# Split weight sums of two pairs of both wide gates formed ahead and kept; weighing of the attention on ScalarE; adds of the output stage's jobs behind the spreading of queries

## The chip, the cores and the metric

One NeuronCore of a Trainium2 chip. The metric is device time of one execution in microseconds (us), median of several. The engines of the core: PE (TensorE, matmuls; PEld is its weight loading), DVE (VectorE), ACT (ScalarE), POOL (GpSimd) and SP (SyncE), which issues most of the DMA transfers. PSUM, where matmuls write, has eight banks of 128x512 floats, here all given out by one pool ("bank").

## The reference

One layer of an encoder on 256 tokens of width 2048, in float32:

```python
h = rms_norm(x, norm_mix)
uv, qkv, gates = split(h @ w_in)
u, v = split(gelu(uv));  v = layer_norm(v)
y_a = u * (w_s @ v + b_s)                   # 8 groups, chunks of 128 tokens
y_b = neighbourhood_attention(q, k, v, rpb) # 16 heads of 64
g_a, g_b = split(sigmoid(gates))            # 2 x 2048 columns
x = x + (g_a * (y_a @ wb_a) + g_b * (y_b @ wb_b)) @ w_out
x = x + (silu(gate) * val) @ w_down         # gate, val: convolved h2 @ w_up, 2 x 5504 columns
out = rms_norm(x, norm_final)
```

## The kernel before

**Numbers.** A float32 value is written as a high and a low part (type fp32r). A product of a piece takes three matmuls: high by high, low by high, high by low. The weights come from DRAM in full and are split in the kernel: ACT copies the high part (`whi`, L165), DVE subtracts it (`wlo`, L166).

**Pieces.** The program goes through some 470 pieces of weights of 256 rows, in a list. `begin(i)` opens piece i: it issues the load of piece i+5 on SP's queue (five raw buffers), splits piece i+3 (four buffers), and then runs the tasks that were hung on number i with `at(i, f)`, those of the construction first. The order of the instructions on every engine is the order in which this Python runs; nothing is reordered, and an engine that waits holds up all that is behind it. So the numbers handed to `at` are the schedule.

**Groups around the change.** v and the attention's v (pieces 0 to 31, wide), u (32 to 47), then by turns a group of q and k (8 pieces, two pairs of heads) and one of a half gate (8 pieces): 48 to 111. Four half branches (112 to 127, four pieces each), the wide halves of gate A (128 to 143) and of gate B (144 to 159), the last branches (160 to 175), the output projection (176 to 207), and then up and down.

**Wide groups and quads.** A wide group has 16 pieces of 256 rows by 512, in eight pairs; a pair is a 256x1024 block of weights. It is worked off plainly (24 matmuls, 2 pieces of 4 products) or as a quad, by block sums that need seven products instead of eight (21 matmuls; 9 in the first piece, 12 in the second). For a quad, four sums of the activations' blocks and four of the weights' blocks must be formed on DVE and split on ACT and DVE. `GATE_QUADS` says which positions of a gate's order are quads, `GATE_ORDER` which rows stand where. A wide group takes four banks for plain products (`C`), and from its first quad on four more for the quads' own products (`P`). In the output stage the split weight sums of some pairs are formed far ahead ("jobs", `split_ahead`): a load `tw` of 1 MB on SP's queue, four adds of 128x512 on DVE (L1226), two splits of 128x1024 (ACT L1231, DVE L1232), and four writes of 512 KB to DRAM, from where they are read back by `split_read` on POOL's queue.

**Mixing.** In the u group, `mix` has PE multiply v into a bank (tasks of pieces 43 to 46 and 51 to 54); DVE adds the bias from it (L684), multiplies u (L685) and splits the result with ACT (L531, L532).

**Attention.** For each pair of heads, in steps hung on piece i: `scores` on PE (L815) from `qs`, `ks` and the low part `kl` that the spreading of queries leaves (DVE L743, L744); one piece later the exponential on ACT (L838); then `weigh`, the division by the sum (DVE L846); at i+5 `turn`, four transpositions on PE (L855) that ACT copies out; at i+8 `apply`.

**Merging.** `ev_branch` multiplies a branch with its gate on DVE and adds the two (L922, L925); `turn_m` transposes the merged column on PE into two banks (L944, four a bank), ACT copies them out (L949, L521) and DVE forms the low parts (L526). The turn of the second merged column is hung on piece 146, the second piece after gate B begins with 144.

Of the kernel before, what the change touches and what calls it, by code (L numbers as in the profile page):

```python
# [73 lines left out]
def trunk_kernel(ctx, tc, x, x_t, vecs, w_in, ln_g, ln_b, w_st, b_s, rpb, w_branch, w_out, w_up, w_down,  # L74
# [204 lines left out]
    def wide(src, row0, order, c0, acts, quads, room, done, sums=None, stored=None, split=None, late=False):  # L279
        n0 = plan_wide(src, row0, order, c0)  # L280
        boxes = {}
        for q in quads:
# [10 lines left out]
            if ready:  # L293
                halved.add(i)
                for n, lead in zip(("13", "24"), ready):
                    at(i - lead, lambda b=b, k=k, n=n: split[1](k // 2, b, n))
                continue
# [263 lines left out]

    def open_y():
        for k in range(KD // 2):
            yT.extend(new_pair(ypool, f"y{k}"))
        ypool.tile([128, Y_GAP // 4], F32, name="gap")


# [235 lines left out]
    def attend(hp, i):  # L803
# [38 lines left out]
        def weigh():  # L842
            sc, sm = box["p"], box["sm"]
            for s in range(2):
                for t in range(NT):
                    nc.vector.tensor_scalar(sc[:, s, t, :], sc[:, s, t, :], sm[:, s, t:t + 1], None, op0=OP.mult)  # L846

# [26 lines left out]
        at(i + 1, soft)  # L874
        at(i + 2, weigh)
        at(i + 5, turn)
# [311 lines left out]
    def g_branch(br, j):  # L1188
# [4 lines left out]
    g_m = [g_branch(1, 0), g_branch(1, 1)]  # L1193
    x_sums, m_sums = ({2 * q: {} for q in qs} for qs in (GATE_KEPT + (GATE_MADE,), OUT_PAIRS))
    g_gw = [wide(w_in2, 0, GATE_ORDER[br], (GA0, GB0)[br] + 1024, xt, GATE_QUADS[br], sums_room,
                 (ev_gate_sums(br), ev_gate_wide(br)), x_sums) for br in range(2)]
    g_m2 = [g_branch(br, j) for j in (2, 3) for br in range(2)]
    out_room = {n: f"h{m}" for m, n in enumerate(("s0", "s1", "s2", "s3", "h13", "l13", "h24", "l24"))}

    def out_sums_room(name, dt):  # L1200
        if name in ("s0", "s1", "s2", "s3"):
            return hpool.tile([128, 2, 512], dt, name=out_room[name])
        return sums_room("l24" if name == "f" else name, dt)

# [9 lines left out]

    def split_ahead(src, kept, room, high, queue, pair, g, load_at, adds, splits, later):
        box = {}

        def load():
            w = box["w"] = room().tile([128, 4, 512], F32, name="tw")
            ld = src.shape[-1]  # L1220
            queue.dma_start(w, bass.AP(tensor=src.tensor, offset=src.offset + pair * 256 * ld + g * 1024,
                                           ap=[[ld, 128], [128 * ld, 2], [1, 1024]]))
# [16 lines left out]
        for i, (d, a, b) in zip(adds, ((0, 0, 1), (1, 1, 3), (3, 0, 3), (2, 2, 3))):  # L1239
            at(i, lambda d=d, a=a, b=b: add(d, a, b))  # L1240
        for i, c, name in zip(splits, (0, 2), ("13", "24")):
# [16 lines left out]
    for n, (pair, g) in enumerate((pair, g) for g in range(2) for pair in OUT_SPLIT[g]):  # L1258
        t_kept[pair, g] = split_rows("out", pair, g)
        i = g_at[2 * n][1]  # L1260
        split_ahead(w_o, t_kept, lambda: at_pool["jobs"], lambda c: f"th{c}", nc.sync, pair, g, i + OUT_JOB[0], [i + a for a in OUT_JOB[1]],
                    [i + a for a in OUT_JOB[2]], 4)
    x_kept = {q: dram.tile([128, 2, 512], F32, name=f"xsums{q}") for q in GATE_KEPT}

    def keep_sums(q):
        nc.gpsimd.dma_start(x_kept[q], first_sums[2 * q]["tile"].bitcast(F32))

    def kept_sums(n, q):
        o = sums_room(f"s{n}", F32R)
        nc.gpsimd.dma_start(o.bitcast(F32), x_kept[q])  # L1270
        x_sums[2 * q]["s"] = sums_of(o)

    for n, q in enumerate(GATE_KEPT):
        at(KEEP_AT[n], lambda q=q: keep_sums(q))
        at(g_gw[0][1] - 4 + n, lambda n=n, q=q: kept_sums(n, q))
    sum_acts_at(g_gw[0][1] - 1, g_gw[0][1] + 1, x_sums[2 * GATE_MADE], lambda: x_pairs[GATE_MADE], sums_room, "s3")
    for n, q in enumerate(OUT_PAIRS):
# [33 lines left out]
    for p, turn in zip(DOWN_SPLIT, DOWN_JOBS):  # L1311
        for g in range(2):
            d_kept[p, g] = split_rows("down", p, g)
            i = g_up[turn[g]][1]
            split_ahead(w_d, d_kept, lambda: ff["more"], lambda c: "so", nc.gpsimd, p, g, i, range(i + 6, i + 10), (i + 10, i + 12), 0)

# [53 lines left out]
    run_group(g_at[0])  # L1370
    G_st.close()
    mg["p"], mg_st = pool("merge", "right")
    mg["fp"], f_st = pool("turned", "right")
    for g in g_at[1:]:
        run_group(g)
    run_group(g_m[0])
    assert at_pool["done"] == HEADS // 2
    at_pool["jobs_st"].close()
    at_pool["st"].close()
    open_m(0)  # L1380
    s_room["p"], s_st = pool("sums")
# [29 lines left out]
    for half in (1, 0):  # L1411
        mg["m_st", half].close()
    turns_st.close()
    fa, fa_st = pool("act")
# [79 lines left out]
```

## Time and profile before

| | us |
|---|---|
| median of 3 runs | 1296.45 (1296.23 to 1296.52) |
| the profiled execution | 1296.47 |
| its span in the trace | 1294.7 |
| granted clock of PE, mean | 0.998 |

The span goes from the first to the last instruction that the profiler recorded; the remaining 1.8 us lie around it. In the profile's rows a time is followed by a duration, the engine, the line (L166 is line 166 of the kernel before), the operation, what it writes and reads, and in brackets the idle time ahead of it with what ended it. A group ends in "xcount | busy us, mean ns of one | idle before". Matmuls are pipelined, so their busy times overlap: 20 in a row take less than 20 times the mean of one.

### The profile page before, as it was taken

How to read it: one execution, taken by the hardware profiler on the slowest of the kernel's cores; microseconds unless marked ns; L12 is line 12 of the kernel's file. 1: busy time of each engine (PE TensorE's matmuls, PEld its weight loads, DVE VectorE, ACT ScalarE, POOL GpSimd, SP SyncE). 2: the span in 40 equal slices, each digit the busy share in tenths (PEclk: the TensorE clock that was granted, in tenths of full speed). 3: DMA queues.
4: the chain of work that ended last, by engine and by line, in shares of the span. 5: the costliest groups of instructions: out<-in, count | busy, mean ns of one | idle time of the engine just before them, and what ended most of it. 6: DMA issues, size and time to landing. Idle time of an engine off the chain costs nothing.

```text
span 1294.7 us, 19576 instructions
## 1 busy us (share of the span) xinstructions
PE 1284.6 (99%) x6668; PEld 1096.2 (85%) x6668; DVE 1124.3 (87%) x1703; ACT 798.9 (62%) x1186; POOL 167.9 (13%) x309
## 2 busy tenths in 40 slices
PE   9999999999999999999999999999999999999997
PEld 7888888888888888888888888888888888888885
DVE  8897778778889888997888899899988989988988
ACT  7766476776755745566566656566665656555654
POOL 0006406323000001100001001100000001211210
PEclk9999999999999999999999999999999999999999
DMA  9789659668677676975598788888877859998993
GB/s 368 271 276 254 194 190 315 227 214 294 224 231 231 193 261 223 411 239 171 173 297 265 241 299 292 269 265 290 264 219 222 278 173 363 366 389 306 362 389 147
DMA packets 192900, 344.86 MB, mean 266 GB/s; under 512 B 15264, under 2 KB 123424, under 8 KB 192800
## 3 DMA queue, kind: packets, MB, share of 16 engines
q1 hardware_dynamic: 168336, 261.33, 60.6%
q0 software_dynamic: 23888, 81.23, 17.9%
q8 instruction: 52, 0.85, 0.3%
q10 hardware_dynamic: 576, 1.06, 0.2%
q14 instruction: 48, 0.39, 0.1%
HBM read 305.80 MB, written 35.65 MB: 264 GB/s over the span
## 4 chain that ended last, share of the span: by engine, by line
PE 99%; DVE 1%; ACT 0%; issue 0%; DVEq 0%
PE bank L217 31%; PE bank L221 16%; PE bank L314 12%; PE bank L312 12%; PE bank L313 12%; PE bank L245 5%; PE bank L247 4%; PE bank L246 4%; PE bank L815 1%; PE bank L865 0%; PE bank L488 0%; PE bank L680 0%; PE bank L944 0%; PE bank L855 0%; PE bank L1019 0%; DVE x L1091 0%
## 5 line engine op out<-in xcount | busy, mean ns | idle before, releaser
L166 DVE TENSOR_TENSOR wlo<-wraw,whi 128x1024 fp32r<-128x1024 f32 (+1 forms) x472 | 540.4, 1159 | 123.7 <-ACT whi L165 83.7
L165 ACT ACTIVATE whi<-wraw 128x1024 fp32r<-128x1024 f32 (+1 forms) x472 | 464.4, 1000 | 208.8 <-PE bank L313 74.5
L217 PE MATMUL bank<-h,whi 128*128 128x512 f32 x1760 | 425.5, 392 | 0.0
L217 PEld LDWEIGHTS bank<-h,whi 128*128 128x128 f32 x1760 | 322.4, 189 | 61.5
L221 PEld LDWEIGHTS bank<-h,wlo 128*128 128x128 f32 x1760 | 226.0, 191 | 8.7
L221 PE MATMUL bank<-h,wlo 128*128 128x256 f32 x1760 | 228.6, 283 | 0.0
L1045 ACT ACTIVATE tc<-ta,ck 128x256 f32<-128x256 f32 x86 | 47.1, 595 | 109.9 <-DVE ta L1043 109.9
L312 PE MATMUL bank<-whi,h 128*128 128x512 f32 x216 | 84.9, 393 | 0.0
L314 PE MATMUL bank<-wlo,h 128*128 128x512 f32 x216 | 84.4, 391 | 0.0
L313 PE MATMUL bank<-whi,h 128*128 128x512 f32 x216 | 84.4, 391 | 0.0
L314 PE MATMUL bank<-wlo,a 128*128 128x512 f32 x188 | 73.5, 391 | 0.0
L312 PE MATMUL bank<-whi,a 128*128 128x512 f32 x188 | 73.3, 390 | 0.0
L313 PE MATMUL bank<-whi,a 128*128 128x512 f32 x188 | 73.2, 390 | 0.0
L1048 DVE SCALAR_TENSOR_TENSOR tc<-ta,ck,tc 128x255 f32<-128x255 f32 x86 | 41.4, 482 | 14.4 <-ACT tc L1045 14.4
L780 POOL TENSOR_SCALAR_AFFINE_SELECT bias<-run 64x128 f32<-64x128 f32 x64 | 39.4, 648 | 101.8 <-DVE sc L823 101.1
L245 PE MATMUL bank<-whi,y 128*128 128x512 f32 x128 | 50.5, 395 | 0.0
L245 PE MATMUL bank<-whi,h 128*128 128x512 f32 x128 | 50.5, 394 | 0.0
L247 PE MATMUL bank<-wlo,h 128*128 128x512 f32 x128 | 50.0, 390 | 0.0
L247 PE MATMUL bank<-wlo,y 128*128 128x512 f32 x128 | 49.9, 390 | 0.0
L246 PE MATMUL bank<-whi,y 128*128 128x512 f32 x128 | 49.9, 390 | 0.0
L246 PE MATMUL bank<-whi,h 128*128 128x512 f32 x128 | 49.9, 390 | 0.0
L1236 POOL DMA_DIRECT2D down_h<-so x16 | 8.6, 539 | 310.9 <-ACT so L1231 179.4
(308 smaller groups left out, 1998.5 us busy)
## 6 DMA issues: line engine op xcount, KB each, us to landing
wraw<-in_w_up_dram SPq DMA_DIRECT2D x336, 256.0 KB, 4.1
wraw<-in_w_in_dram SPq DMA_DIRECT2D x111, 512.0 KB, 5.1
wraw<-in_w_down_dram SPq DMA_DIRECT2D x78, 512.0 KB, 7.8
wraw<-in_w_in_dram SPq DMA_DIRECT2D x66, 256.0 KB, 3.8
wraw<-in_w_branch_dram SPq DMA_DIRECT2D x32, 512.0 KB, 4.8
wraw<-in_w_out_dram SPq DMA_DIRECT2D x28, 512.0 KB, 6.6
h<-sums POOLq DMA_DIRECT2D x18, 512.0 KB, 8.6
tw<-in_w_down_dram POOLq DMA_DIRECT2D x8, 1024.0 KB, 8.6
```

The lines of the kernel that those rows point to most:

```text
L165: nc.scalar.activation(h[:, k, :m], w[:, k, :m], AF.Copy)
L166: nc.vector.tensor_sub(l[:, k, :m], w[:, k, :m], h[:, k, :m].bitcast(F32))
L217: nc.tensor.matmul(p, h[:, k - k0, b * 128:(b + 1) * 128], acts(k), start=k == 0, stop=k == nk - 1)
L221: nc.tensor.matmul(p[:, :T], l[:, k - k0, b * 128:(b + 1) * 128], acts(k)[:, 0, :], start=False, stop=False)
L245: nc.tensor.matmul(p, xh, h[:, kk, :m], start=st, stop=False)
L246: nc.tensor.matmul(p, xl, h[:, kk, :m], start=False, stop=False)
L247: nc.tensor.matmul(p, xh, l[:, kk, :m], start=False, stop=sp)
L312: nc.tensor.matmul(p, xh, h, start=st, stop=False)
L313: nc.tensor.matmul(p, xl, h, start=False, stop=False)
L314: nc.tensor.matmul(p, xh, l, start=False, stop=sp)
L1045: nc.scalar.activation(v, u, AF.Identity, scale=ck[:, 1, ch:ch + 1], bias=ck[:, 3, ch:ch + 1])
L1048: nc.vector.scalar_tensor_tensor(v[:, 1:], u[:, :T - 1], ck[:, 0, ch:ch + 1], v[:, 1:], op0=OP.mult, op1=OP.add)
```

## The change

Nothing of what is computed changes. More pairs of both wide gates become quads: positions 0, 1, 2, 4, 5, 6 of gate A in place of 0, 2, 4, 6, and 1, 2, 4, 5, 6 of gate B in place of 2, 4, 6. For pairs 0 and 3 of both gates the split weight sums are made by jobs far ahead, as in the output stage, written to DRAM and read back into tiles `kh`, `kl`: the first job in the u and first q,k groups (load at piece 40, adds at 44, 46, 48, 48, splits at 49 and 51), the others in the q,k groups 64, 80 and 96, beside the jobs of the output stage. All six activation sums that the gates use are kept in DRAM and read by both gates, eleven reads in place of three; those of pairs 0 and 3 are made at pieces 38 and 39 in rooms that later hold `y4` to `y7`, and that of pair 4 at 116 in place of 127. `weigh` goes from DVE to ACT, and one piece later. The adds of the output stage's jobs go from 12, 12, 13 and 14 pieces behind a group's begin to 15, behind the task that spreads the queries.

```diff
-GATE_KEPT, GATE_MADE = (1, 2, 6), 4
-GATE_QUADS = ((0, 2, 4, 6), (2, 4, 6))
-GATE_ORDER = ((2, 3, 0, 1, 4, 5, 6, 7, 12, 13, 10, 11, 8, 9, 14, 15), (0, 1, 6, 7, 2, 3, 10, 11, 4, 5, 14, 15, 12, 13, 8, 9))
+GATE_KEPT, GATE_MADE = (1, 2, 6), (0, 3, 4)
+GATE_QUADS = ((0, 1, 2, 4, 5, 6), (1, 2, 4, 5, 6))
+GATE_ORDER = ((2, 3, 0, 1, 4, 5, 10, 11, 12, 13, 6, 7, 8, 9, 14, 15), (10, 11, 0, 1, 2, 3, 14, 15, 4, 5, 6, 7, 12, 13, 8, 9))
+GATE_SPLIT = ({0: (4, 6, 5), 3: (4, 6, 6)}, {0: (4, 6, 6), 3: (4, 6, 6)})
+GATE_FIRST = (40, (44, 46, 48, 48), (49, 51))
+GATE_JOB = (3, (6, 6, 7, 7), (9, 12))
+GATE_SUMS = ((0, 38, 40, "y4", "y5"), (3, 39, 40, "y6", "y7"))
+GATE_LATE, Y_LATE = 4, 44
...
-OUT_JOB = (10, (12, 12, 13, 14), (17, 20))
+OUT_JOB = (10, (15, 15, 15, 15), (17, 20))
...
-                    nc.vector.tensor_scalar(sc[:, s, t, :], sc[:, s, t, :], sm[:, s, t:t + 1], None, op0=OP.mult)
+                    nc.scalar.activation(sc[:, s, t, :], sc[:, s, t, :], AF.Copy, scale=sm[:, s, t:t + 1])
...
-        at(i + 2, weigh)
+        at(i + 3, weigh)
...
+    def kept_sums(pair, box):
+        o = sums_room(f"s{gate_turn[0]}", F32R)
+        gate_turn[0] = (gate_turn[0] + 1) % 3
+        nc.gpsimd.dma_start(o.bitcast(F32), x_kept[pair])
+        box["s"] = sums_of(o)
+
+    g_gw = [wide(w_in2, 0, GATE_ORDER[br], (GA0, GB0)[br] + 1024, xt, GATE_QUADS[br], sums_room,
+                 (ev_gate_sums(br), ev_gate_wide(br)), stored=kept_sums,
+                 split=(GATE_SPLIT[br], split_read(g_kept, br, lambda pair, name: sums_room("k" + name, F32R))))
+            for br in range(2)]
...
+    for n, (pair, br) in enumerate((pair, br) for br in range(2) for pair in GATE_SPLIT[br]):
+        g_kept[pair, br] = split_rows("gate", pair, br)
+        i, (a, b, c) = (g_at[2 * n][1], GATE_JOB) if n else (0, GATE_FIRST)
+        split_ahead(w_in2, g_kept, lambda: at_pool["jobs"],
+                    lambda c: f"th{c}", nc.sync, pair, br, (GA0, GB0)[br] + 1024, i + a, [i + k for k in b],
+                    [i + k for k in c], 3, "jobs2" if n else "jobs")
...
-    sum_acts_at(g_gw[0][1] - 1, g_gw[0][1] + 1, x_sums[2 * GATE_MADE], lambda: x_pairs[GATE_MADE], sums_room, "s3")
+    def sums_job(q, i, j, tiles):
+        box = {}
+
+        def sums():
+            w, box["o"] = tiles()
+            box["w"], a = w, x_pairs[q]
+            f = w[:, 0].rearrange("p (k t) -> p k t", k=2)
+            nc.vector.tensor_add(f, a[:, :, 0, :].bitcast(F32), a[:, :, 1, :].bitcast(F32))
+            act_blocks(w[:, 1], *(f[:, k, t * 128:(t + 1) * 128] for k in range(2) for t in range(2)))
+
+        def split():
+            w, o = box["w"], box["o"]
+            nc.scalar.activation(o[:, 0], w[:, 1], AF.Copy)
+            nc.vector.tensor_sub(o[:, 1], w[:, 1], o[:, 0].bitcast(F32))
+
+        at(i, sums)
+        at(j, split)
+        at(j + 2, lambda: nc.gpsimd.dma_start(x_kept[q], box["o"].bitcast(F32)))
...
+    for q, i, j, w, o in GATE_SUMS:
+        sums_job(q, i, j, lambda w=w, o=o: in_y((w, o)))
+    sums_job(GATE_MADE[-1], g_at[8][1] + GATE_LATE, g_at[8][1] + GATE_LATE + 1, in_jobs)
```

What this moves is seen in the engines' lists. A row has its number in the engine's list, the line, the operation, and what is written and read; line numbers of the changed kernel differ (L171 there is L166 here, L697 is L684, L869 is L856, L859 is the weighing, L957 is L944, L317 to L319 are L312 to L314).

DVE in the second half of the u group, where the bank of the mixing is read (L684, L697), before:

```order
119 L166 TENSOR_TENSOR wlo<-wraw,whi 128x1024
120 L532 TENSOR_TENSOR y_1140<-ya,y_1140 128x256
121 L684 TENSOR_TENSOR ya<-bank,bsb 128x128 x2
122 L685 TENSOR_TENSOR ya<-ya,u_1232 128x256
123 L532 TENSOR_TENSOR y_1140<-ya,y_1140 128x256
124 L166 TENSOR_TENSOR wlo<-wraw,whi 128x1024
125 L684 TENSOR_TENSOR ya<-bank,bsb 128x128 x2
126 L685 TENSOR_TENSOR ya<-ya,u_1233 128x256
127 L532 TENSOR_TENSOR y_1141<-ya,y_1141 128x256
...
131 L532 TENSOR_TENSOR y_1141<-ya,y_1141 128x256
132 L166 TENSOR_TENSOR wlo<-wraw,whi 128x1024
133 L669 TENSOR_TENSOR ta<-bank,tb 128x256 x4
134 L651 TENSOR_TENSOR ta<-ta,rb 128x256 x4
135 L166 TENSOR_TENSOR wlo<-wraw,whi 128x1024 x4
136 L684 TENSOR_TENSOR ya<-bank,bsb 128x128 x2
```

and with the change, where the first gate job's adds are L1250:

```order
133 L171 TENSOR_TENSOR wlo<-wraw,whi 128x1024
134 L1250 TENSOR_TENSOR tw<-tw 128x512
135 L537 TENSOR_TENSOR y_1159<-ya,y_1159 128x256
136 L697 TENSOR_TENSOR ya<-bank,bsb 128x128 x2
137 L698 TENSOR_TENSOR ya<-ya,u_1261 128x256
138 L537 TENSOR_TENSOR y_1159<-ya,y_1159 128x256
...
143 L171 TENSOR_TENSOR wlo<-wraw,whi 128x1024
144 L1250 TENSOR_TENSOR tw<-tw 128x512
145 L697 TENSOR_TENSOR ya<-bank,bsb 128x128 x2
...
152 L1250 TENSOR_TENSOR tw<-tw 128x512 x2
153 L171 TENSOR_TENSOR wlo<-wraw,whi 128x1024
154 L1256 TENSOR_TENSOR tw<-tw,th_1623 128x1024
```

One add stands ahead of the first split of a mixed group, and one ahead of the last reading of the bank; two more and the subtraction of the job (L1256) follow ahead of the first q,k group's mixing.

ACT ahead of the last turn of the attention (`pT` copies out the transpositions), before:

```order
236 L838 ACT_TABLE_LOAD
237 L838 ACTIVATE sc,sm<-sc,mx 128x128 x4
238 L165 ACTIVATE whi<-wraw 128x1024
239 L1231 ACTIVATE th_3877<-tw 128x1024
240 L165 ACTIVATE whi<-wraw 128x1024 x3
241 L856 ACTIVATE pT<-bank 128x512
```

and with the change, where L1317 splits the activation sums of pair 4:

```order
265 L851 ACT_TABLE_LOAD
266 L851 ACTIVATE sc,sm<-sc,mx 128x128 x4
267 L170 ACTIVATE whi<-wraw 128x1024
268 L1255 ACTIVATE th_3983<-tw 128x1024
269 L170 ACTIVATE whi<-wraw 128x1024
270 L1317 ACTIVATE tw<-tw 128x512
271 L859 ACTIVATE sc<-sc,sm 128x128 x4
272 L170 ACTIVATE whi<-wraw 128x1024 x2
273 L869 ACTIVATE pT<-bank 128x512
```

The weighing and the split of the sums are now between the exponential and the copy.

PE in gate B, from the transpositions of the merged column to the first quad, whose products of weight sums (tiles `h`, `l`, or `kh`, `kl` where they are read back) by activation sums `s` go to the banks `P`, before:

```order
1371 L944 MATMUL bank<-ident,g_2614 128x128 x8
1372 L312 MATMUL bank<-whi,h_112 128x512
...
1399 L312 MATMUL bank<-whi,h_110 128x512
1400 L313 MATMUL bank<-whi,h_110 128x512
1401 L314 MATMUL bank<-wlo,h_110 128x512
1402 L312 MATMUL bank<-whi,s_4072 128x512
1403 L313 MATMUL bank<-whi,s_4072 128x512
1404 L314 MATMUL bank<-wlo,s_4072 128x512
1405 L312 MATMUL bank<-h_4585,s_4072 128x512
```

and with the change:

```order
1365 L957 MATMUL bank<-ident,g_2688 128x128 x8
1366 L317 MATMUL bank<-whi,h_109 128x512
...
1371 L319 MATMUL bank<-wlo,h_109 128x512
1372 L317 MATMUL bank<-whi,s_4623 128x512
1373 L318 MATMUL bank<-whi,s_4623 128x512
1374 L319 MATMUL bank<-wlo,s_4623 128x512
1375 L317 MATMUL bank<-kh_4582,s_4623 128x512
1376 L318 MATMUL bank<-kh_4582,s_4623 128x512
1377 L319 MATMUL bank<-kl_4583,s_4623 128x512
1378 L317 MATMUL bank<-kh_4582,s_4623 128x512
```

The 24 matmuls of a plain pair between the transpositions and the quad are gone: the second and third of the products with sums stand 9 and 12 matmuls behind the transpositions (rows 1375 and 1378), where it was 33 and 36.

More of the change, by code (lines that the diff above doesn't have):

```diff
@@ L294, in wide @@
                 halved.add(i)
-                for n, lead in zip(("13", "24"), ready):
+                for n, lead in zip(("13", "24"), ready[-2:]):
                     at(i - lead, lambda b=b, k=k, n=n: split[1](k // 2, b, n))
@@ L1193, in trunk_kernel @@
     g_m = [g_branch(1, 0), g_branch(1, 1)]
[L1194 to L1203, printed above, removed]
+    m_sums = {2 * q: {} for q in OUT_PAIRS}
+    g_kept, x_kept = {}, {}
+    gate_turn = [0]
     def split_read(kept, g, tile_of):
@@ L1239, in split_ahead @@
         for i, (d, a, b) in zip(adds, ((0, 0, 1), (1, 1, 3), (3, 0, 3), (2, 2, 3))):
-            at(i, lambda d=d, a=a, b=b: add(d, a, b))
+            if last:
+                at(i - 1, lambda i=i, d=d, a=a, b=b: at(i, lambda: add(d, a, b)))
+            else:
+                at(i, lambda d=d, a=a, b=b: add(d, a, b))
         for i, c, name in zip(splits, (0, 2), ("13", "24")):
@@ L1260, in trunk_kernel @@
         i = g_at[2 * n][1]
-        split_ahead(w_o, t_kept, lambda: at_pool["jobs"], lambda c: f"th{c}", nc.sync, pair, g, i + OUT_JOB[0], [i + a for a in OUT_JOB[1]],
-                    [i + a for a in OUT_JOB[2]], 4)
-    x_kept = {q: dram.tile([128, 2, 512], F32, name=f"xsums{q}") for q in GATE_KEPT}
+        split_ahead(w_o, t_kept, lambda: at_pool["jobs"], lambda c: f"th{c}", nc.sync, pair, g, g * 1024, i + OUT_JOB[0], [i + a for a in OUT_JOB[1]],
+                    [i + a for a in OUT_JOB[2]], 4, last=True)
```

38 lines of the change are left out of this document (27 added, 11 removed).

## The prediction

> **What bounds the kernel now.** I read the page's first part, then the waits of the tensor engine (PE), then the chain that ended last.
>
> ```profile
> span 1294.7 us, 19576 instructions
> PE 1284.6 (99%) x6668; PEld 1096.2 (85%) x6668; DVE 1124.3 (87%) x1703; ACT 798.9 (62%) x1186; POOL 167.9 (13%) x309
> PEclk9999999999999999999999999999999999999999
> PE bank L488 <- DVE one L478: 1.5, 1, 1.5
> 1.47 4.02 PE bank L488 x9
> 136.43 4.56 PE bank L217 x20
> ```
>
> PE is busy for 99% of the span, it waits once (1.5 us, at the start), and its granted clock stays in the top tenth. So the kernel ends when PE has run through its list: a matmul that goes is time gained, and any wait that the change gives to PE is time lost. There is no third way, except over the clock. What one matmul is worth must not be read from its busy time. The groups give 393 ns to a 128x512 matmul, but they overlap: the last line has 20 of them in 4.56 us, 0.228 us each.
>
> **What the change takes away.** Quads rise from 4 and 3 pairs to 6 and 5, four more; a quad has 21 matmuls where a plain pair has 24. 4 x 3 = 12 matmuls of 128x512 fall away: 12 x 0.228 = **2.7 us**. By the mean busy time it would be 12 x 0.393 = 4.7, which is wrong for the reason just given. Against the profiled run (1296.47 us, 1.8 us more than its span; the median of the runs is 1296.45, the same) this alone gives 1293.7.
>
> **What it adds, and where that is late.** All additions lie on DVE, ACT and the queues. They cost nothing as long as a buffer, a bank or an operand is ready before PE wants it, so I looked for those with the least lead. The order shown with the change has three places.
>
> *First place: the u group and the first head.* VectorE (DVE) gets two sums of activations, two subtractions, four adds of weights and two more subtractions between 113 us and 162 us. The rows of before:
>
> ```profile
> 117.40 1.23 DVE L166 TENSOR_TENSOR wlo<-wraw,whi 128x1024 fp32r<-128x1024 f32 x1 [1.65 <-ACT whi L165]
> 120.09 1.23 DVE L166 TENSOR_TENSOR wlo<-wraw,whi 128x1024 fp32r<-128x1024 f32 x1 [1.46 <-ACT whi L165]
> 123.69 2.46 DVE L166 TENSOR_TENSOR wlo<-wraw,whi 128x1024 fp32r<-128x1024 f32 x2 [2.37 <-ACT whi L165]
> ...
> 135.30 1.31 DVE L166 TENSOR_TENSOR wlo<-wraw,whi 128x1024 fp32r<-128x1024 f32 x1 [0.47 <-DMA wraw<-in_w_in_dram]
> 136.54 0.48 DVE L684 TENSOR_TENSOR ya<-bank,bsb 128x128 f32<-128x128 f32 x2
> ...
> 148.06 1.23 DVE L166 TENSOR_TENSOR wlo<-wraw,whi 128x1024 fp32r<-128x1024 f32 x1 [1.79 <-PE bank L221]
> 154.55 1.23 DVE L166 TENSOR_TENSOR wlo<-wraw,whi 128x1024 fp32r<-128x1024 f32 x1 [0.98 <-PE bank L221]
> 168.99 0.42 DVE L744 TENSOR_TENSOR kl<-ta,ks 64x256 fp32r<-64x256 f32 x1
> 378.30 0.69 DVE L330 TENSOR_TENSOR f<-h 128x512 f32<-128x512 f32 x1
> 380.09 1.28 DVE L922 TENSOR_TENSOR g<-bank,g 128x512 f32<-128x512 f32 x2
> L1226 DVE TENSOR_TENSOR tw<-tw 128x512 f32<-128x512 f32 x16 | 11.0, 686 | 0.1
> 136.26 2.46 PE L217 MATMUL bank<-h,whi 128*128 128x512 f32 x10
> 170.00 0.27 PE L815 MATMUL bank<-kl,qs 128*128 128x160 f32 x1
> ```
>
> A sum of activations takes 1.8 us (378.30, where before made the one of pair 4, to 380.09). The two, with two subtractions of 512 at 0.65 (a 128x512 add has a mean of 0.686, a little less where they overlap), are 4.9 us, and the idle time ahead of the three splits at 117 to 124 us is 1.65 + 1.46 + 2.37 = 5.5 us. I call that hidden: 0, with up to 0.6 us left over since the gaps and the work don't lie side by side. After 126 us the cover is gone. The remaining gaps (0.5 us) are DVE and ScalarE (ACT) answering each other, which no other work can fill for nothing. Two adds, 1.3 us, now stand ahead of the last row that reads the mixing bank (136.54 + 0.48 = 137.02). Four of the ten matmuls of 136.26 close the old group, and the next four open the four banks of the new one; the fourth needs the bank just freed, at 136.26 + 7 x 0.228 = 137.85. Lead 0.83. The late part of the load of 1 MB is an unknown: the DMA engines are full from 105 to 125 us,
>
> ```profile
> 120.00:125.00 5.00, 5.00 (x35) 4.59 (x34) 2.54 (x3) 4.97 (x9) 3.88 (x8) 1.00 1.07 347
> 130.00:140.00 10.00, 10.00 (x60) 8.85 (x60) 6.96 (x12) 4.92 (x9) 9.75 (x20) 1.00 0.65 180
> ```
>
> (two stretches; the last numbers are the clock, the DMA share and GB/s: 1.07 and 347), so 1.05 MB push what is behind them on SP's queue back by 3.0 us, most of which is worked off by 135 us at a share of 0.65. I take 0.3 us as left, between 0 and 0.6. Shift 1.6, stall at the first q,k piece **0.8 us** (0 to 1.1; 0 if the gaps of 0.5 take the adds after all).
>
> Behind it come two more adds (1.3) and two subtractions of 1024 (1.14 each, below), and gaps of 1.79 and 0.98 where DVE waits for PE give 2.8 back: 1.6 + 1.3 + 2.3 - 2.8 = 2.4 us at the scores of the first head. Their second kl is ready at 169.41 and read at 170.00, lead 0.59. So PE is 1.8 us late by then, of which 0.8 is spent: **1.0 us** more (0 to 1.4). From 160 to 335 us the other gate jobs share pieces with OUT jobs; there DVE meets PE again in waits, and I price them at nothing, up to 1 us if the spreading's gap is too short.
>
> *Second place: the turn of the scores before piece 119.* The factor of softmax now runs on ACT, a piece later, and behind the split of pair 4's activation sums, which themselves come behind an OUT job on DVE.
>
> ```profile
> 347.41 1.22 DVE L1232 TENSOR_TENSOR tw<-tw,th 128x1024 fp32r<-128x1024 f32 x1
> 348.55 0.86 DVE L846 TENSOR_SCALAR sc<-sc,sm 128x128 f32<-128x128 f32 x4
> 343.32 0.40 ACT L838 ACTIVATE sc<-sc,mx 128x128 f32<-128x128 f32 x1 [1.31 <-DVE mx L829]
> 346.78 1.04 ACT L165 ACTIVATE whi<-wraw 128x1024 fp32r<-128x1024 f32 x1
> 350.82 0.60 PE L855 MATMUL bank<-ident,sc 128*128 128x128 f32 x4
> ```
>
> DVE ends its subtraction at 348.55 (1.14 after its start), forms the sums until 350.34, ACT splits 512 columns of them (0.63, as the row of 421.02 below) until 350.97, and then weighs four times 128x128. Before, DVE had that done at 349.41, 1.4 us ahead of PE. No row has this operation on ACT; the nearest is the exponential on the same tile, 0.40 us. Four take 1.2 (0.3 apart where they overlap, as the exponential's next instruction starts 0.31 later) to 1.6, so the last is ready at 352.2 to 352.6. The last of the four transpositions was at 351.1: **1.1 us** of stall (0.6 to 1.5; queued behind the weighing on ACT are only splits with a piece of lead). The Trainium skill, ScalarE: Activation LUTs, section What ACT_TABLE_LOAD costs, gives 186 ns and 0.833 ns a column, 93 ns more for a factor by pointer, and 93 ns of overlap, by which four would take an estimated 1.3 us and the stall be 1.2. At the other heads ACT has no such split ahead of it, and the turn is two pieces behind the weighing: 0.
>
> *Third place: the first quad of gate B.* It moves from the third pair to the second, so it follows right on the transpositions of the merged column. Two of the four product banks it takes are those that the transpositions just filled.
>
> ```profile
> 423.77 1.03 PE L944 MATMUL bank<-ident,g 128*128 128x128 f32 x8
> 424.56 0.48 PE L312 MATMUL bank<-whi,h 128*128 128x512 f32 x1
> 432.82 0.39 PE L312 MATMUL bank<-h,s 128*128 128x512 f32 x1
> 421.02 0.63 ACT L165 ACTIVATE whi<-wraw 128x512 fp32r<-128x512 f32 x1 [1.66 <-PE bank L313]
> 422.96 2.20 ACT L911 ACTIVATE g<-g,n_r 128x1024 f32<-128x1024 f32 x2
> 426.01 1.99 ACT L369 ACTIVATE h<-t 128x1024 fp32r<-128x1024 f32 x2
> 428.39 0.63 ACT L521 ACTIVATE m<-bank 128x256 fp32r<-128x256 f32 x2
> 427.28 2.35 DVE L370 TENSOR_TENSOR l<-t,h 128x1024 fp32r<-128x1024 f32 x2
> 429.56 1.41 DVE L526 TENSOR_TENSOR m<-bank,m 128x256 fp32r<-128x256 f32 x4
> ```
>
> The four DVE rows at 429.56 read these banks, two each, so the first is free at about 430.3 (half of 1.41 us) and the other at 431.0. Before, the products that start those banks stood at 432.82 and one triple later: 2.5 us of lead. In the new order the first comes 12 matmuls behind the transpositions, at 424.56 + 12 x 0.228 = 427.3. What DVE waits for is a chain on ACT (sigmoids of gate A, a split, two splits of 1024 columns, the copies of the bank) which starts with a wait for PE at 421.02 and has no gap, and it is the same in the new order. Hence **3.0 us** (430.3 - 427.3); the next bank is wanted 0.7 us after the first and free 0.7 after it, so it adds nothing. Bounds 2 (if ACT gains a microsecond, since the split of a first half there is shorter now) and 3.3.
>
> *At nothing.* Adds of the OUT jobs behind the spreading: the same count, in gaps. One sum of 1.8 us leaves gate A's DVE. Eight kept reads more and the kept weight sums go through POOL's queue, six pieces ahead:
>
> ```profile
> 421.00:463.00 42.00, 42.00 (x191) 34.86 (x191) 37.33 (x47) 26.93 (x32) 1.84 (x4) 1.00 0.65 196
> 520.00:552.00 32.00, 32.00 (x142) 26.51 (x142) 29.24 (x37) 16.12 (x19) 6.38 (x11) 1.00 1.02 409
> h<-sums POOLq DMA_DIRECT2D x18, 512.0 KB, 8.6
> ```
>
> Gate B moves 196 GB/s; eight tiles (4.2 MB) and five activation sums (2.6 MB) more over 42 us make it some 360, under the 409 of the output stage, where PE has no wait. A read lands in 8.6 us and is asked for at least five pieces of nine matmuls ahead, 10 us. If that cover went, each microsecond that a tile is late would be one lost.
>
> **Sum.** 1296.5 - 2.7 + 0.8 + 1.0 + 1.1 + 3.0 = **1299.7**.
>
> **Rivals.**
> - *The covers hold* (faster). DVE's gaps of 0.5 us take the adds, ACT weighs in time, and the chain ahead of the merged banks gets shorter. Against it: three leads of 0.6 to 2.5 us that I find overdrawn by 1 to 3. It needs all three. 1293.7; chance 0.1.
> - *Only the banks at gate B stall* (no change). For it: it is the one wait whose two ends are both in the trace, while the other two rest on shifts that I summed over 50 us, or on an operation not in the trace. 1296.5 - 2.7 + 3.0 = 1296.8; with one half of the others up to 1298. Chance 0.25.
> - *A stall costs twice, by the clock.* The nine matmuls at the start took 4.02 us, 0.45 each, which is half speed behind an idle PE. Nine such again after the 3.0 us stall would add 9 x 0.22 = 2.0: 1301.7. Against it: no such stall in this trace. Chance 0.07. The Trainium skill, TensorE: Matmul & The Clock Gate, Part 1, has the clock halve after an idle window of about 3.4 us whose phase is free; a stall of 3.0 us stays below it, so by that rule the rival doesn't come.
> - *Transfers.* The full DMA engines of 105 to 125 us hold up the pieces behind the load by its 3.0 us, or gate tiles land late: 1302 to 1304. Chance 0.08.
> - My own sum, 1298 to 1301.5: chance 0.5.
>
> **Numbers.** A measurement here tells 0.2% (2.6 us) from no change, that is 1293.9 to 1299.0. Faster: the first rival, 0.10. Same: the second, and the part of mine below 1299.0, 0.25 + 0.05. Slower: the rest, 0.60. The range of 1296 to 1302.3 leaves out the first rival and the upper half of the transfers; the likeliest case by itself has 1298 to 1301.5.
>
> **What would show it.** PE's waits, which were one, should be three or four: a matmul of the first q,k group behind the mixing, about 138 us, and a score matmul near 171, for DVE; a transposition near 353 for ACT, of 1 us; and a product of the second pair of gate B near 431 for DVE or ACT, of 3 us, the longest. If that last one is missing I have the banks wrong; if PE waits for a DMA, the transfers were it; if neighbouring starts behind a wait stand 0.45 apart, it is the clock.

## The result and the profile after

The change made the kernel slower: 1303.24 us (median of 4 runs, 1302.41 to 1306.78) against 1296.34 (4 runs, 1296.19 to 1296.52), a ratio of 1.0058 with a 95% interval of 1.0040 to 1.0077. The forecast was 1299.7, in a range of 1296.0 to 1302.3: the sign was right, the loss was 6.9 us in place of 3.4, and the time lies above the range. The profiled execution is the fastest of the four, 1302.41 us.

The page of the changed kernel, its first parts, and the waits of PE (engine and line, what it waited for, us in all, times, longest):

```profile
span 1300.6 us, 19691 instructions
PE 1285.2 (99%) x6656; PEld 1094.2 (84%) x6656; DVE 1140.3 (88%) x1707; ACT 813.2 (63%) x1228; POOL 186.1 (14%) x336
```

```profile
PE bank L317 <- DVE m L531: 2.9, 1, 2.9
PE bank L493 <- DVE one L483: 1.5, 1, 1.5
PE bank L828 <- ACT ks L755: 1.4, 2, 0.9
PE bank L868 <- ACT sc L859: 0.6, 1, 0.6
PE bank L319 <- DVE wlo L171: 0.5, 1, 0.5
```

The 12 matmuls are gone (6668 to 6656), and where PE had one wait it has six. The waits add up to 5.4 us without the one at the start, which with 2.7 us gained would make the span 2.7 longer; it is 5.9 longer. A wait row gives only the time in which PE had nothing to do, and neither the pipeline that runs dry around it nor what follows. So the starts of the matmuls have to be read. The timeline of PE after, at the scores of the first head and the first product behind them, at the turn, and at gate B:

```profile
169.25 0.39 PE L252 MATMUL bank<-wlo,h 128*128 128x512 f32 x1
170.56 0.34 PE L828 MATMUL bank<-ks,qs 128*128 128x160 f32 x1 [0.92 <-ACT ks L755]
171.97 0.34 PE L828 MATMUL bank<-ks,qs 128*128 128x160 f32 x1 [0.46 <-ACT ks L755]
172.77 0.43 PE L250 MATMUL bank<-whi,h 128*128 128x512 f32 x1
...
353.01 0.39 PE L252 MATMUL bank<-wlo,y 128*128 128x512 f32 x1
354.02 1.21 PE L868 MATMUL bank<-ident,sc 128*128 128x128 f32 x4 [0.62 <-ACT sc L859]
354.98 0.49 PE L250 MATMUL bank<-whi,y 128*128 128x512 f32 x1
...
429.61 0.39 PE L319 MATMUL bank<-kl,s 128*128 128x512 f32 x1
432.90 0.47 PE L317 MATMUL bank<-kh,s 128*128 128x512 f32 x1 [2.90 <-DVE m L531]
434.42 0.63 PE L317 MATMUL bank<-kh,h 128*128 128x512 f32 x1
434.84 0.63 PE L318 MATMUL bank<-kh,h 128*128 128x512 f32 x1
437.77 0.40 PE L319 MATMUL bank<-wlo,h 128*128 128x512 f32 x1
```

and of before, the products around the first two of these places:

```profile
169.25 0.39 PE L247 MATMUL bank<-wlo,h 128*128 128x512 f32 x1
170.33 0.44 PE L245 MATMUL bank<-whi,h 128*128 128x512 f32 x1
...
350.59 0.39 PE L247 MATMUL bank<-wlo,y 128*128 128x512 f32 x1
351.18 0.48 PE L245 MATMUL bank<-whi,y 128*128 128x512 f32 x1
```

Up to 169.25 us the two run level. The first head then costs 172.77 - 170.33 = 2.4 us, the turn (354.98 - 353.01) - (351.18 - 350.59) = 1.4, and gate B 3.29 between two starts that should be 0.23 apart, 3.1. Right behind that, the starts stand 0.42 apart (434.42, 434.84) until 437.77: eight of them take 3.35 us in place of 1.8, 1.5 us more. This is PE at half its clock: the granted clock is 0.50 from 434.3 to 437.7 us. The sum: -2.7 + 2.4 + 1.4 + 3.1 + 1.5 = 5.7, and 6.2 with the wait of 0.5 us near the end (L319, for a split); the spans differ by 5.9, so the readings are good to some 0.3 us.

Why each came so late is seen in DVE and ACT after. First the rows of DVE on the way to the first head, then those of ACT at the turn, then DVE at gate B:

```profile
137.11 0.47 DVE L697 TENSOR_TENSOR ya<-bank,bsb 128x128 f32<-128x128 f32 x2
152.55 0.48 DVE L697 TENSOR_TENSOR ya<-bank,bsb 128x128 f32<-128x128 f32 x2
157.46 1.23 DVE L171 TENSOR_TENSOR wlo<-wraw,whi 128x1024 fp32r<-128x1024 f32 x1 [0.53 <-ACT whi L170]
171.83 0.42 DVE L757 TENSOR_TENSOR kl<-ta,ks 64x256 fp32r<-64x256 f32 x1
...
432.01 1.41 DVE L531 TENSOR_TENSOR m<-bank,m 128x256 fp32r<-128x256 f32 x4
```

```profile
353.04 0.63 ACT L1317 ACTIVATE tw<-tw 128x512 fp32r<-128x512 f32 x1 [2.62 <-DVE tw L326]
353.58 1.27 ACT L859 ACTIVATE sc<-sc,sm 128x128 f32<-128x128 f32 x4
```

The last reading of the mixing's bank moved from 136.54 to 137.11 only, in time for PE; the kl of the first head from 168.99 to 171.83. ACT stood still for 2.6 us ahead of the split of pair 4's sums, with the weighing behind it. And the m rows of gate B end where the bank is freed, at 432.7 for the first.

### The profile page after: what moved, and what is told of

Read it like the earlier page. It is cut to its first block, busy times and chain, and to the rows that moved or that the text cites. A ratio compares the mean times of both kernels' runs of the same rounds, so it can differ in the third digit from the quotient of the medians.

```text
span 1300.6 us, 19691 instructions
## 1 busy us (share of the span) xinstructions
PE 1285.2 (99%) x6656; PEld 1094.2 (84%) x6656; DVE 1140.3 (88%) x1707; ACT 813.2 (63%) x1228; POOL 186.1 (14%) x336
## 3 DMA queue, kind: packets, MB, share of 16 engines
q10 hardware_dynamic: 576, 1.06, 0.2%
## 4 chain that ended last, share of the span: by engine, by line
PE 64%; DVE 1%; DMA 1%; issue 0%; ACT 0%; DVEq 0%; SPq 0%
PE bank L222 24%; PE bank L226 13%; PE bank L319 8%; PE bank L317 8%; PE bank L318 8%; PE bank L251 1%; PE bank L250 1%; PE bank L252 1%; DMA wraw<-in_w_down_dram 1%; DVE wlo L171 1%; PE bank L1032 0%; DVE h L375 0%; PE bank L957 0%; DVE h L364 0%; ACT x L1158 0%
## 5 line engine op out<-in xcount | busy, mean ns | idle before, releaser
L171 DVE TENSOR_TENSOR wlo<-wraw,whi 128x1024 fp32r<-128x1024 f32 (+1 forms) x472 | 537.4, 1151 | 111.5 <-ACT whi L170 78.0
L317 PE MATMUL bank<-whi,h 128*128 128x512 f32 x192 | 75.5, 393 | 0.0
L319 PE MATMUL bank<-wlo,h 128*128 128x512 f32 x192 | 75.3, 392 | 0.2
L318 PE MATMUL bank<-whi,h 128*128 128x512 f32 x192 | 75.3, 392 | 0.0
L319 PE MATMUL bank<-wlo,a 128*128 128x512 f32 x188 | 73.5, 391 | 0.5 <-DVE wlo L171 0.5
L317 PE MATMUL bank<-whi,a 128*128 128x512 f32 x188 | 73.2, 390 | 0.0
L1061 DVE SCALAR_TENSOR_TENSOR tc<-ta,ck,tc 128x255 f32<-128x255 f32 x86 | 41.4, 481 | 14.4 <-ACT tc L1058 14.4
L250 PE MATMUL bank<-whi,h 128*128 128x512 f32 x128 | 50.4, 394 | 0.0
L252 PE MATMUL bank<-wlo,h 128*128 128x512 f32 x128 | 50.0, 390 | 0.0
L251 PE MATMUL bank<-whi,h 128*128 128x512 f32 x128 | 49.9, 390 | 0.0
```

The costliest lines, as they stand in the source:

```text
L171: nc.vector.tensor_sub(l[:, k, :m], w[:, k, :m], h[:, k, :m].bitcast(F32))
L250: nc.tensor.matmul(p, xh, h[:, kk, :m], start=st, stop=False)
L251: nc.tensor.matmul(p, xl, h[:, kk, :m], start=False, stop=False)
L252: nc.tensor.matmul(p, xh, l[:, kk, :m], start=False, stop=sp)
L317: nc.tensor.matmul(p, xh, h, start=st, stop=False)
L318: nc.tensor.matmul(p, xl, h, start=False, stop=False)
```

## The experiments

Each ran in alternation with the kernel before (medians 1296.16 to 1296.36), at another time than the changed kernel's 1303.2, so a difference to that one is between two series of runs. Theory and rivals stand in the words on record.

### Gate B: the turn a piece earlier

```diff
-                at(i + 1 if j == 3 else g_gw[1][1] + 2 if j == 1 else i + 2, lambda: turn_m(j))
+                at(i + 1 if j == 3 else g_gw[1][1] + 1 if j == 1 else i + 2, lambda: turn_m(j))
```

> The turn of the second merged column is hung on piece 145 in place of 146; the rest is the changed kernel (1303.2 us). Theory: the 3.06 us at gate B are the two banks that the transpositions still hold when the first quad wants them, and the slow stretch of 1.75 us behind it comes from that stall. Then the copies run before the sigmoids, the banks are free about 3 us sooner, both losses go, up to 0.5 us may be left for weight sums that are split later: about 1298.4, no PE wait over 1 us in gate B and no starts 0.42 us apart. Rival, ACT and DVE are simply too full there: a wait of 2 us or more stays at another operand, 1301.5 or more. Rival, the slow stretch has nothing to do with the stall: the wait goes and 0.42 us spacing still shows somewhere, 1300.2.

1299.18 us (11 runs, 1297.48 to 1302.57), ratio 1.0024 (1.0015 to 1.0032): 4.1 us less than the change as made, of 4.8 expected. The waits of PE in its profiled execution, which is the slowest of the 11:

```profile
PE bank L222 <- DVE ya L697: 3.2, 1, 3.2
PE bank L868 <- ACT sc L859: 1.8, 1, 1.8
```

and the row of its PE timeline at the mixing's bank:

```profile
141.27 4.83 PE L222 MATMUL bank<-h,whi 128*128 128x512 f32 x13 [3.18 <-DVE ya L697]
```

No wait is left at gate B and no slow stretch either, so the banks it was. But the bank of the mixing, which the changed kernel's profile had in time, is late by 3.2 us here, and the 13 matmuls behind it take 4.83 us, 0.37 each in place of 0.23: PE was at half its clock for most of them. Eight more at half the clock follow the 1.8 us at the turn. The two stretches of DMA ahead of the mixing's end, in before, after and this kernel in this order (clock, share and GB/s are the last three numbers):

```profile
125.00:130.00 5.00, 5.00 (x30) 4.33 (x29) 4.82 (x9) 0.97 (x2) 4.82 (x10) 1.00 0.79 247
130.00:135.00 5.00, 5.00 (x33) 4.49 (x33) 3.31 (x6) 2.46 (x4) 4.81 (x10) 1.00 0.63 177
```

```profile
125.00:130.00 5.00, 5.00 (x30) 4.32 (x29) 4.83 (x11) 1.25 (x2) 2.11 (x5) 1.00 1.02 314
130.00:135.00 5.00, 5.00 (x33) 4.49 (x32) 3.21 (x7) 2.51 (x4) 4.04 (x9) 1.00 0.99 331
```

```profile
125.00:130.00 5.00, 5.00 (x30) 4.32 (x29) 3.27 (x5) 2.09 (x3) 1.25 (x4) 1.00 1.05 394
130.00:135.00 5.00, 5.00 (x34) 4.49 (x33) 3.50 (x7) 2.02 (x4) 4.10 (x9) 1.00 1.04 324
```

With the change the DMA engines stay full 10 us longer, and in this execution a raw piece lands too late for the mixing: at 129.32 us, 14.4 after its issue, where the changed kernel's trace has it at 124.38. The load of the first gate job alone doesn't fill them, since without that job (the experiment on the first head, below) the shares of these stretches are 1.02 and 1.06. What makes the piece late in one execution and not in another is not shown. The changed kernel's run of 1306.78 has no trace; its granted clock on record is 0.993, some 18 us of its span at half speed in place of 10 in the profiled run (0.996), so it had more slow stretches, and which wait led to them stays open.

### Gate B: the quads a position later

```diff
-GATE_QUADS = ((0, 1, 2, 4, 5, 6), (1, 2, 4, 5, 6))
-GATE_ORDER = ((2, 3, 0, 1, 4, 5, 10, 11, 12, 13, 6, 7, 8, 9, 14, 15), (10, 11, 0, 1, 2, 3, 14, 15, 4, 5, 6, 7, 12, 13, 8, 9))
+GATE_QUADS = ((0, 1, 2, 4, 5, 6), (2, 3, 4, 5, 6))
+GATE_ORDER = ((2, 3, 0, 1, 4, 5, 10, 11, 12, 13, 6, 7, 8, 9, 14, 15), (10, 11, 14, 15, 0, 1, 2, 3, 4, 5, 6, 7, 12, 13, 8, 9))
```

> Gate B's quads stand at positions 2 to 6 in place of 1, 2, 4, 5 and 6, the plain pair of rows 14 and 15 goes to position 1, so the first quad is where it was before the change; the count of matmuls is the changed kernel's. Theory of the banks: both the 3.06 us and the slow stretch of 1.75 us go, about 1298.4. Rival, a gate that is short of DVE time or of kept tiles: the wait moves to a later pair (two quads with sums on DVE now follow each other) and 1.5 us or more stay, 1300 or more.

1299.7 us (9 runs), ratio 1.0024 (1.0014 to 1.0033). Much the same gain by another way (3.5 us): no bank wait, no slow stretch at gate B. What keeps it above the 1298.4 of the theory is in its profile: a slow stretch of 3.4 us at another place, behind the first head (its two waits are 1.27 and 0.45 us here), and 0.8 us in which PE waits for a read of kept sums:

```profile
PE bank L317 <- DMA s<-xsums: 0.8, 1, 0.8
```

### The turn: the split of pair 4's sums a piece later

```diff
-    sums_job(GATE_MADE[-1], g_at[8][1] + GATE_LATE, g_at[8][1] + GATE_LATE + 1, in_jobs)
+    sums_job(GATE_MADE[-1], g_at[8][1] + GATE_LATE, g_at[8][1] + GATE_LATE + 2, in_jobs)
```

> The split of pair 4's activation sums is hung on piece 118 in place of 117, so behind the weighing of the last heads; the rest is the changed kernel (1303.2 us). Theory: weighing on ACT is late only because that split, which waits for DVE, stands ahead of it; the 1.4 us at the turn go, about 1301.8, with no wait of a transposition on ACT. Rival, weighing on ACT is late by itself (four times 0.39 us, a piece later): 0.7 us or more of the wait stays, 1302.5.

1302.35 us (5 runs, 1300.83 to 1303.95), ratio 1.0044 (1.0030 to 1.0057). The time alone would not tell the two theories apart; the waits do:

```profile
PE bank L317 <- DVE m L531: 2.9, 1, 2.9
PE bank L828 <- ACT ks L755: 1.6, 2, 1.2
```

No transposition waits any more. Weighing on ACT is in time by itself; what made it late was the split ahead of it. The profiled execution (1303.32) is no faster than the changed kernel's all the same, since its clock is at half for 10.2 us in place of 3.4: 3.4 behind the first head, where there was no slow stretch, and 6.8 at gate B.

### The first head: the first gate job left out

```diff
-GATE_QUADS = ((0, 1, 2, 4, 5, 6), (1, 2, 4, 5, 6))
-GATE_SPLIT = ({0: (4, 6, 5), 3: (4, 6, 6)}, {0: (4, 6, 6), 3: (4, 6, 6)})
+GATE_QUADS = ((0, 2, 4, 5, 6), (1, 2, 4, 5, 6))
+GATE_SPLIT = ({3: (4, 6, 6)}, {0: (4, 6, 6), 3: (4, 6, 6)})
...
-    for n, (pair, br) in enumerate((pair, br) for br in range(2) for pair in GATE_SPLIT[br]):
+    for n, (pair, br) in enumerate(((pair, br) for br in range(2) for pair in GATE_SPLIT[br]), 1):
```

> Pair 0 of gate A is a plain pair, its job (load at piece 40, four adds, two splits, writes) is left out, and the other three jobs stay where they are; three more matmuls, 0.7 us. Theory: the wait of 2.4 us at the first head's scores is the DVE work of that job on a chain without slack, so it goes: 1303.2 - 2.4 + 0.7 = 1301.5, and no PE wait near 170 us. Rival, the two activation sums at pieces 38 and 39 or the extra transfers shift the chain: 1 us or more of the wait stays, 1302.5 or more.

1302.12 us (5 runs), ratio 1.0044 (1.0031 to 1.0056). In its profile the wait at the first head is gone altogether, gate B (2.9) is as it was, and the turn waits 1.0 in place of 0.6. So the job, and neither the two activation sums nor the kept reads, made it. Its time is 0.6 us above what was expected.

### Which part of the job

The kernel has the turn on piece 145 and the split of pair 4's sums on 118, as above. Of the first gate job it leaves out what DVE does, so that the weight sums of gate A's pair 0 are not formed:

```diff
-            nc.vector.tensor_add(w[:, d], w[:, a], w[:, b])
+            if load_at != 40:
+                nc.vector.tensor_add(w[:, d], w[:, a], w[:, b])
...
-            nc.vector.tensor_sub(w.bitcast(F32R), w, h.bitcast(F32))
+            if load_at != 40:
+                nc.vector.tensor_sub(w.bitcast(F32R), w, h.bitcast(F32))
```

> The changed kernel with the turn on piece 145 and the split of pair 4's sums on 118; of the first gate job (still at piece 40) the four adds and two subtractions on DVE are left out, so its weight sums are not formed (gate A's pair 0 is wrong), while its load, ACT's two splits, the four writes and all matmuls stay. Theory: the 2.4 us at the first head's scores are that DVE work alone (shift 2.9 us, 5.0 us of work): no such wait, about 1293.7 in most runs, with a run now and then some us slower when the full DMA engines make a raw piece late at the mixing (seen once: 3.2 us and a slow stretch). Rival: the transfers or ACT's two splits make it: 1 us or more of the wait stays, 1295 or more in all runs.

1293.44 us (11 runs, 1293.02 to 1294.08), ratio 0.9978 (0.9970 to 0.9987). PE's waits:

```profile
PE bank L493 <- DVE one L483: 1.5, 1, 1.5
PE bank L319 <- DVE wlo L171: 0.4, 1, 0.4
```

The transfers and ACT's two splits cost nothing here: the 2.4 us are the adds and subtractions on DVE. No run of the eleven is above 1294.08 us, so no late raw piece cost some us either, although the DMA engines are as full in the trace:

```profile
125.00:130.00 5.00, 5.00 (x30) 4.32 (x29) 4.83 (x10) 1.94 (x3) 1.81 (x4) 1.00 1.06 397
130.00:135.00 5.00, 5.00 (x33) 4.49 (x32) 3.00 (x7) 2.71 (x4) 3.71 (x9) 1.00 1.09 374
```

So full DMA engines alone do not make PE wait; in this trace the raw piece landed at 125.55 us. This is also the measure of the 12 matmuls: 1296.36 - 1293.44 = 2.9 us.

### All three mended

All three have the turn on piece 145 and the split of pair 4's sums on 118. First with the job behind the first head, and the other jobs' loads and adds a piece later, to make room in the tile they share:

```diff
-GATE_FIRST = (40, (44, 46, 48, 48), (49, 51))
-GATE_JOB = (3, (6, 6, 7, 7), (9, 12))
+GATE_FIRST = (57, (60, 60, 60, 60), (61, 62))
+GATE_JOB = (4, (7, 7, 7, 7), (9, 12))
...
-                    [i + k for k in c], 3, "jobs2" if n else "jobs")
+                    [i + k for k in c], 3, "jobs2")
```

> The changed kernel with three edits: turn of the second merged column on piece 145, split of pair 4's sums on 118, and the first gate job moved behind the first head (load at piece 57, adds at 60, splits at 61 and 62, in the second room; the other three jobs' loads and adds a piece later). Theory: the three places are all there is, so 1296.3 - 2.7 = 1293.6 if the job finds cover there; its 4.9 us of DVE against some 3 us of gaps between 169 and 186 us may leave up to 1.5 us at the second head's scores: 1293.6 to 1295.1, faster than before. Rival: DVE from 160 to 340 us has no room for a fourth job: waits of PE at the scores of later heads, 1296 or more.

1294.83 us (11 runs), ratio 0.9988 (0.9979 to 0.9997). No slow stretch is left but the one at the start; two waits at the scores are:

```profile
PE bank L828 <- ACT g L904: 0.7, 2, 0.4
```

Then with the job left out:

> As the former, but pair 0 of gate A stays a plain pair and its job is left out; 9 matmuls fewer than before in place of 12 (2.0 us). Theory: no wait is left at the three places: 1296.3 - 2.0 = 1294.3, up to 0.5 more. Rival: what is left of the edits (weighing on ACT, two activation sums early, eight kept reads) costs by itself: 1296 or more.

1294.79 us (11 runs), ratio 0.9988 (0.9980 to 0.9997): nine matmuls fewer and no wait before the end of the kernel, so the same time as the former. And with the job behind the first head, but `GATE_JOB` as the change has it:

> The three edits with the first gate job behind the first head (load at 57, adds at 60), but the other three jobs where the change has them. In three_edits_job_later the waits of 0.5 us (second head) and 0.7 us (second q,k group) were left. Theory: the second came from putting the others a piece later, so 1294.2 here, and the wait of 0.5 us at the second head stays. Rival: SP's queue holds the next load until the first job's writes are done and raw pieces come late: 1295.5 or more.

1294.35 us (11 runs, 1293.73 to 1295.56), ratio 0.9985 (0.9976 to 0.9993): **the fastest version with nothing left out, 0.15% under the kernel before**, with all 12 matmuls saved. Its one new wait is 0.3 us at the second head; the theory had 0.5 there.

### What the two moves are worth

On the version with the job left out (1294.79), the weighing was put back on DVE, and the output stage's adds back to their old places:

```diff
-                    nc.scalar.activation(sc[:, s, t, :], sc[:, s, t, :], AF.Copy, scale=sm[:, s, t:t + 1])
+                    nc.vector.tensor_scalar(sc[:, s, t, :], sc[:, s, t, :], sm[:, s, t:t + 1], None, op0=OP.mult)
...
-        at(i + 3, weigh)
+        at(i + 2, weigh)
```

> three_edits_job_left_out (1294.8) with the weighing back on DVE two pieces behind the scores. Theory: moving it to ACT frees 0.86 us a head on DVE, which only matters where DVE has a short lead (scores behind gate jobs): 1294.8 to 1296.3. Rival: the move was of no use, same time; or ACT's lists were the tighter ones, then faster, 1294.3.

```diff
-OUT_JOB = (10, (15, 15, 15, 15), (17, 20))
+OUT_JOB = (10, (12, 12, 13, 14), (17, 20))
```

> three_edits_job_left_out (1294.8) with the output stage's adds back at 12, 12, 13 and 14 pieces. Theory: 2.6 us of adds ahead of the spreading make the scores of every second head late where the lead is 0.6 to 1.6 us, on top of the gate jobs: waits at the scores in groups 64, 80 and 96, 1295.5 to 1297. Rival: the gaps of the spreading don't bind, same time.

1297.73 us (ratio 1.0010, 1.0001 to 1.0019) and 1296.83 (1.0005, 0.9996 to 1.0014): 2.9 and 2.0 us lost. The waits of PE, of the first and of the second:

```profile
PE bank L868 <- DVE sc L859: 1.9, 3, 1.3
```

```profile
PE bank L828 <- ACT g L904: 1.0, 1, 1.0
```

The longest of the first, 1.3 us, is at the last turn. DVE there:

```profile
351.86 0.69 DVE L1312 TENSOR_TENSOR tw<-h 128x512 f32<-128x512 f32 x1
...
353.65 0.48 DVE L859 TENSOR_SCALAR sc<-sc,sm 128x128 f32<-128x128 f32 x2
```

The sums of pair 4 stand ahead of the weighing (1.8 us), so that it is late on DVE too; the expectation had left that out, and 2.9 us are twice the most it allowed. The second came out as the theory had it, with one wait at the scores of 1.0 us in place of three; by the starts of its matmuls, some 0.6 us more is lost at the last turn. Both moves carry cover that the other gate jobs and pair 4's sums need.

### How long a wait costs the clock

In the kernel before, 16 waits of PE in the up projection, by matmuls of zeros around clearings on POOL:

```diff
+    def hold(k):
+        p = bank()
+        nc.tensor.matmul(p[:, :128], junk[:, :128], junk[:, :128], start=True, stop=True)
+        for _ in range(k):
+            nc.gpsimd.memset(junk, 0.0)
+        nc.tensor.matmul(p[:, :128], junk[:, :128], junk[:, :128], start=True, stop=True)
+
+    for n in range(16):
+        at(g_up[n + 3][1] + 4, lambda k=n % 8 + 1: hold(k))
```

> The kernel before, with PE held on purpose 16 times in the up projection: one matmul of zeros, one to eight clearings of a 128x512 tile by GpSimd, and a matmul that reads it, twice each size. Nothing of the output changes. Theory: a wait of PE well below 3.4 us can already cost a slow stretch (starts 0.43 us apart for about 3.4 us, 1.7 us lost), with some chance that grows with the wait. Then some of the waits of 1 to 3 us are followed by such a stretch, and all of 4 us and more. Rival: only a wait of 3.4 us or more does; then none of the shorter ones is, and the slow stretch at gate B had another cause.

One run, 1434.73 us. The sizes came out unevenly (seven of the sixteen waits had POOL's transfers ahead of the clearings, 8 us more). PE around the shortest and the next longer wait, each followed by one group of 16 matmuls of 128x512:

```profile
669.28 0.49 PE L1322 MATMUL bank<-junk 128*128 128x128 f32 x2 [0.71 <-POOL junk L1321]
669.53 3.90 PE L217 MATMUL bank<-h,whi 128*128 128x512 f32 x16
...
728.32 0.49 PE L1322 MATMUL bank<-junk 128*128 128x128 f32 x2 [1.87 <-POOL junk L1321]
728.56 5.51 PE L217 MATMUL bank<-h,whi 128*128 128x512 f32 x16
```

After 0.71 us the sixteen take 3.90 us, after 1.87 they take 5.51: 1.6 us more. Both waits of 0.7 us left the clock alone; each of the fourteen of 1.87 us or more (to 12.9) was followed by a stretch of starts 0.43 us apart. Four of the fourteen are below 3.4 us (two of 1.87, two of 3.03), so the rival, that only waits of 3.4 us or more do this, is out.

## Why the prediction fell short, point by point

**What bounds the kernel, and the gain.** Right: PE's list is the time, and 12 x 0.228 = 2.7 us is what the matmuls are worth (2.9 in the run without waits).

**First place.** Right in its cause, DVE's work for the first job on a chain without slack, and in the place where it ends, the first head; wrong in its parts. "Stall at the first q,k piece 0.8 us" was 0 in the profile: the last reading of the bank moved by 0.57 us, not 1.6. The first add (0.7) was absorbed ahead of 134.3 us, and not in an idle time: two rows of DVE (127.02, 133.09) had taken 1.49 and 0.78 us before and took 1.22 and 0.42 after. Why they were longer before is not shown, so that the add cost nothing there is luck. "Most of which is worked off by 135 us" was wrong, since the DMA engines stayed full until then; one traced execution of another version had a late raw piece and a wait of 3.2 us there, which the job's load is not shown to have caused. At the head the sum gave 2.4 us of shift and it was 2.84 (171.83 - 168.99): of the gap of 0.98 at 154.55, which I counted in full, only 0.44 came back (152.55 was 149.20 before, a shift of 3.35, and 157.46 was 154.55, one of 2.91). So 2.4 us in place of 1.8.

**Second place.** Right, 1.4 us for 1.1. ACT's split waited as worked out (2.6 us idle, for the sums' last row), and the four weighings took 1.27 us, between the 1.2 and 1.6 of the bounds. The Trainium skill, ScalarE: Activation LUTs, section What ACT_TABLE_LOAD costs, led to an estimate of 1.3, with which this agrees.

**Third place.** Right: 3.0 us forecast, 3.1 between the starts; the bank, the rows of DVE and the chain on ACT are those named.

**At nothing.** In the changed kernel the kept reads and the other gate jobs cost nothing, as said. But I called the adds behind the spreading free without asking what they free: they, and the weighing on ACT, were worth 2.0 and 2.9 us when taken back.

**Transfers.** The fourth rival, 1302 to 1304, has the measured time in its range, but by chance: in the profile PE waits for no transfer.

**The step that failed** is the third rival, "a stall costs twice, by the clock", to which I gave 0.07. The price (2.0 us for nine matmuls) was near what was paid: 1.5 in the profile, and as much in the probe. The sign named for it, neighbouring starts 0.45 apart behind a wait, came (0.42). The mistake was to leave it out of the sum because the stalls were under 3.4 us. The Trainium skill, TensorE: Matmul & The Clock Gate, Part 1, has the clock halve after an idle window of about that length. The traces agree with steps of that length (the last section), but not with it as a least wait: 2.90 us were followed by half speed in all three traces that have it, and 1.87 us were, each time, in the probe. With the 1.5 us, the sum 1299.7 would have become 1301.2, within 1.2 us of the profiled run; most of these are the first place (0.6 more than in the sum), the turn (0.3) and the wait of 0.5 near the end. The remaining 0.8 to the median lies in executions that are not in a trace.

## What to carry to other kernels

Where one engine is the time, saved instructions are worth their spacing, and every microsecond of lateness beyond a lead is lost; so price a change by the shortest leads it overdraws, bank by bank, and count a gap of another engine as cover only if nothing else answers across it. An instruction that waits should not stand ahead of one that is wanted (the split of sums ahead of the weighing), and a quad that takes banks should not follow right on what filled them. Waits of PE that add up to 1.6 us or more within some 3.4 us should be charged 1.5 us more for the clock, two short ones as well as a long one.

## What the runs showed of the hardware that was not expected

PE's clock falls to half for about 3.4 us after waits much shorter than that: 14 of 14 waits of 1.87 us or more in the probe, none of two of 0.7. In the kernels the length of a single wait doesn't settle it: waits of 0.6, 1.0 and 1.3 us at transpositions were not followed by it, and one of 1.8 was; two waits in a row at the first head (0.92 and 0.46 us) were not, but 1.27 and 0.45, and 1.15 and 0.46, were.

The clock records of the traces show what does. Within a trace all slow stretches begin on one grid of 3.41 us and last one to four of its steps (3.41, 6.83, 10.24, 13.65 us); where the grid lies differs from execution to execution. With PE's idle time added up within each step, every step at full clock with 1.61 us or more was followed by one at half clock, and none with 1.47 us or less was, in all thirteen traces (the start, which the records don't cover, left out). The steps of the first head, of the changed kernel and then of the version with the quads a position later (stretch, its length, PE's busy time, and as above the clock, share and GB/s last):

```profile
168.05:171.46 3.41, 2.41 (x11) 1.56 (x10) 2.61 (x6) 2.31 (x5) 0.00 (x0) 1.00 0.88 304
171.46:174.87 3.41, 2.87 (x14) 2.32 (x14) 2.60 (x4) 3.36 (x5) 0.00 (x0) 1.00 0.09 31
```

```profile
169.10:172.51 3.41, 1.61 (x9) 0.86 (x7) 2.60 (x7) 2.80 (x7) 0.00 (x0) 1.00 0.79 279
172.51:175.92 3.41, 3.41 (x10) 2.81 (x11) 2.63 (x4) 2.88 (x3) 0.00 (x0) 0.50 0.05 14
```

In the first the two waits fall into two steps, in the second into one, with 1.80 us idle, and the next step runs at 0.50. Within a step already at half clock less was enough for another: 0.71 us at gate B of the version with the later split, where the slow stretch is 6.8 us long. This is counted from the traces; no run moved a wait across the grid on purpose.

Full DMA engines (shares of 0.99 to 1.09 from 125 to 135 us) cost PE 0.5 us or less at the mixing in five traces, and 3.2 us in a sixth.
